# The S5 half of an output projection as seven block products instead of eight, its factors formed on the way

## The chip, the core and the metric

One Trainium2 chip, one core of it. The metric is the device time of one execution in microseconds (us), the median of several runs. The engines are PE (TensorE, matrix products), DVE (VectorE), ACT (ScalarE), POOL (GpSimd) and SP (SyncE, which here issues nearly all the DMAs). Each engine works through its own list of instructions in order, and semaphores make one wait for another.

## The reference, cut to what matters

One layer of a streaming encoder over 544 frames (512 of a new stream, 32 of a running one), width 2048, all in float32:

```python
h = rmsnorm(x, norm1_g)
q, f, i, g, u = split(h @ w_in)            # 4 x 1024 columns for HGRN2, 1024 for S5
o_h, S = hgrn_mixer(q, f, i, g, ...)       # 8 heads of 128, a gated linear recurrence
y = s5_ssm(u) ; hh = gelu(y)
o_s = hh * sigmoid(hh @ w_glu + b_glu)     # the GLU
mix = concatenate([o_h, o_s])              # 2048 channels
x = x + mix @ w_out                        # the output projection: (2048 x 2048)
x = x + square(relu(rmsnorm(x, norm2_g) @ w_ff1)) @ w_ff2
y = rmsnorm(x, final_norm_g)
```

The change is in `o_s @ w_out[1024:]`, the S5 half of the output projection: 1024 channels in, 2048 out.

## The kernel before

All products run transposed: channels lie on the 128 partitions and the frames along the free dimension, in two halves of 272 (`HALF`). A float32 product is made of three passes of the tensor engine: both factors are split into a rounded part and the rest (`hi` and `lo`), and `step` (L124 to L126) issues hi x hi, hi x lo and lo x hi, each 128 x 128 by 272 columns. A weight block is 128 x 1024 (eight K tiles for one block of 128 outputs): SP loads it (L88), ACT casts `hi` (L108) and DVE subtracts to `lo` (L109). Raw weights (`w`) and split ones (`hl`) have rings of two buffers each.

The stages, in order: input projection with the S5 and HGRN2 mixers woven into it; the GLU (eight blocks of 48 matmuls); the S5 half of the output projection (16 blocks of 48 matmuls, called here the S5 stage); the HGRN2 half (the HG stage, 16 blocks of 48); then the FFN, whose two products already use the seven-product scheme (`seven`, with eight PSUM banks).

In the GLU each block's result passes a sigmoid (ACT, L58) and a product with its input (DVE, L1001), and `split` (L184, L185) makes the pair of tiles that the S5 stage multiplies. In the S5 stage each block adds two PSUM banks to tiles `xr`, which hold the input x (L1019 loads, L1022 adds, L1023 stores to a buffer `x2` in HBM). The banks `g` are three.

Beside the S5 stage runs the last HGRN2 head (`hg_head`, head 7). Its matmuls are set between the products by `tick`, which counts pairs of K tiles, so that PE's order is fixed by the program; `manual_schedule` keeps PE to that order. The order on DVE, ACT and SP is made by a list scheduler when the program is built, by its own cost model, with priority for what stands in `with self.first()` (weights). Two steps of the head matter below: `kh` (L669 on DVE), which PE transposes (L679), and `ATs` (L792 on DVE), which PE multiplies (L802).

Before the HG stage the eight heads' outputs are loaded again (`mhl`, L1031, from buffers `mh` in HBM), cast (L1033) and subtracted (L1034) into the eight tiles `mix0` to `mix7`, the factors of that stage. `mhl` tiles come from a ring of four (`x_tile`). In the kernel before nothing else uses that ring in the S5 stage, and the tiles `xr` come from another one (`tt`). The last addition and the last stores of the S5 stage are put behind the first weights of the HG stage (`late_adds`, `stores`).

## Time and profile before

| | us |
|---|---|
| median of 3 runs | 2281.62 |
| the runs | 2277.82 to 2285.32 |
| span of the profiled execution (first to last instruction) | 2276.6 |
| PE busy in it | 2248.7 (99%) |
| DVE busy | 1799.9 (79%) |
| ACT busy | 1288.1 (57%) |
| the S5 stage, from the GLU's last matmul to the HG stage's first | 106.91 |
| of it, busy: PE, DVE, ACT | 106.91, 62.14, 43.51 |

The profiled execution's own time beyond its span is not listed; the median of the runs lies 5.0 us above that span. The profile is read by stages. A matmul's listed duration (about 290 ns) is longer than the distance to the next one (about 126 ns), since matmuls are pipelined, and the same holds in a smaller measure for DVE and ACT: what an instruction costs its engine in a dense stretch is the distance from its start to the next start.

### The profile page before, as it was taken

Reading aid. Unit: us, or ns where it says so; the run is one execution under the profiler, and the core shown is the slowest. Engines: PE = TensorE matmul, PEld = TensorE weight load, DVE = VectorE, ACT = ScalarE, POOL = GpSimd, SP = SyncE. Lnnn points to the kernel's source line nnn. Section 1 sums busy time; section 2 is a strip of 40 time slices with the busy share of each in tenths; the row PEclk is TensorE's granted clock in tenths of the full one; section 3 lists DMA queues with packets and bytes.
Section 4 is the critical chain, followed back from the end, with each engine's and each line's share of the span. In section 5 each row is a group of like instructions: output and inputs, shape, how many; then the busy total and the mean of one; then the engine's idle time right before and its main releaser. Section 6 shows DMA issues by size and latency. Waiting matters only on the chain.

```text
span 2276.6 us, 46775 instructions
## 1 busy us (share of the span) xinstructions
PE 2248.7 (99%) x19310; PEld 2225.2 (98%) x19310; DVE 1799.9 (79%) x2933; ACT 1288.1 (57%) x2259; POOL 39.1 (2%) x59
## 2 busy tenths in 40 slices
PE   8999999999999999999999999999999999999998
PEld 8999999999999999999999999999999999999997
DVE  7988889787657478777777777778888888888896
ACT  5655656564655256555555555556566565565574
POOL 0010001000000000000000000000000000000000
PEclk9999999999999999999999999999999999999999
DMA  5222232222345565445555544447554344344333
GB/s 195 88 83 92 88 91 87 81 84 86 119 146 177 161 201 173 146 157 166 179 169 171 177 147 154 145 143 257 169 173 162 109 164 163 111 162 168 107 103 107
DMA packets 139926, 322.12 MB, mean 141 GB/s; under 512 B 13344, under 2 KB 66336, under 8 KB 139712
## 3 DMA queue, kind: packets, MB, share of 16 engines
q1 hardware_dynamic: 139072, 316.90, 42.9%
q8 instruction: 151, 2.47, 0.5%
q10 hardware_dynamic: 640, 2.23, 0.3%
q14 instruction: 63, 0.52, 0.1%
HBM read 262.21 MB, written 56.87 MB: 140 GB/s over the span
## 4 chain that ended last, share of the span: by engine, by line
PE 90%; DVE 6%; ACT 3%; DMA 1%; issue 1%; SPq 0%; ACTq 0%; DVEq 0%
PE g L124 9%; PE g L126 9%; PE g L125 8%; PE bX L1134 8%; PE bX L1135 8%; PE bX L1136 8%; PE bE L1135 3%; PE bE L1134 3%; PE bC L1135 3%; PE bC L1134 3%; PE bD L1135 3%; PE bD L1134 3%; PE bF L1134 3%; PE bF L1135 3%; PE bD L1136 3%; PE bC L1136 3%
## 5 line engine op out<-in xcount | busy, mean ns | idle before, releaser
L124 PE MATMUL g<-a,hl 128*128 128x272 f32 x1648 | 491.0, 298 | 6.4 <-ACT hl L108 6.4
L126 PE MATMUL g<-a,hl 128*128 128x272 f32 x1648 | 476.0, 289 | 1.3 <-DVE hl L109 1.2
L125 PE MATMUL g<-a,hl 128*128 128x272 f32 x1648 | 475.0, 288 | 0.0
L109 DVE TENSOR_TENSOR hl<-w,hl 128x1024 fp32r<-128x1024 f32 (+3 forms) x348 | 383.5, 1111 | 112.7 <-ACT hl L108 112.2
L108 ACT CAST hl<-w 128x1024 fp32r<-128x1024 f32 (+3 forms) x348 | 334.5, 962 | 201.5 <-PE g L126 117.3
L109 DVE TENSOR_TENSOR hl<-s,hl 128x1024 fp32r<-128x1024 f32 x256 | 313.0, 1223 | 108.6 <-ACT hl L108 108.2
L108 ACT CAST hl<-s 128x1024 fp32r<-128x1024 f32 x256 | 268.7, 1050 | 179.1 <-PE bD L1136 97.9
L124 PEld LDWEIGHTS g<-a,hl 128*128 128x128 f32 x1648 | 311.6, 189 | 10.0 <-ACT hl L108 6.6
L126 PEld LDWEIGHTS g<-a,hl 128*128 128x128 f32 x1648 | 311.1, 189 | 2.3 <-DVE hl L109 2.3
L125 PEld LDWEIGHTS g<-a,hl 128*128 128x128 f32 x1648 | 311.0, 189 | 0.8 <-DVE a L188 0.5
L1135 PE MATMUL bX<-hf,hl 128*128 128x272 f32 x768 | 222.7, 290 | 0.0
L1134 PE MATMUL bX<-f,hl 128*128 128x272 f32 x768 | 222.3, 290 | 0.3 <-ACT hl L108 0.3
L1135 PE MATMUL bX<-f,hl 128*128 128x272 f32 x768 | 222.6, 290 | 0.0
L1134 PE MATMUL bX<-hf,hl 128*128 128x272 f32 x768 | 222.1, 289 | 0.5 <-ACT bD L1127 0.5
L1136 PE MATMUL bX<-f,hl 128*128 128x272 f32 x768 | 221.6, 289 | 0.7 <-DVE hl L109 0.7
L1136 PE MATMUL bX<-hf,hl 128*128 128x272 f32 x768 | 221.3, 288 | 0.0
L1136 PEld LDWEIGHTS bX<-f,hl 128*128 128x128 f32 x768 | 144.5, 188 | 1.0 <-DVE hl L109 1.0
L1134 PEld LDWEIGHTS bX<-hf,hl 128*128 128x128 f32 x768 | 144.7, 188 | 0.7 <-ACT bD L1127 0.7
L1134 PEld LDWEIGHTS bX<-f,hl 128*128 128x128 f32 x768 | 144.7, 188 | 0.6 <-ACT hl L108 0.5
L1136 PEld LDWEIGHTS bX<-hf,hl 128*128 128x128 f32 x768 | 144.5, 188 | 0.0
L1135 PEld LDWEIGHTS bX<-f,hl 128*128 128x128 f32 x768 | 144.4, 188 | 0.0
L1135 PEld LDWEIGHTS bX<-hf,hl 128*128 128x128 f32 x768 | 144.4, 188 | 0.0
(426 smaller groups left out, 5777.3 us busy)
## 6 DMA issues: line engine op xcount, KB each, us to landing
w<-w SPq DMA_DIRECT2D x256, 512.0 KB, 4.0
w<-wi SPq DMA_DIRECT2D x76, 512.0 KB, 3.4
hd<-ft SPq DMA_DIRECT2D x32, 952.0 KB, 4.7
hf<-hd SPq DMA_DIRECT2D x56, 544.0 KB, 6.6
w<-wo SPq DMA_DIRECT2D x32, 512.0 KB, 4.1
x<-x SPq DMA_DIRECT2D x32, 272.0 KB, 2.8
hhl<-hh SPq DMA_DIRECT2D x16, 274.0 KB, 3.5
x<-xT SPq DMA_DIRECT2D x16, 272.0 KB, 5.0
```

The lines of the kernel that those rows point to most:

```text
L108: self.nc.scalar.copy(hi[:, cols], w[:, cols])
L109: self.last_lo = self.nc.vector.tensor_sub(lo[:, cols], w[:, cols], hi[:, cols].bitcast(F32)).ins.name
L124: te.matmul(o, wh, xh, start=k == 0, stop=False)
L125: te.matmul(o, wh, xl, start=False, stop=False)
L126: te.matmul(o, wl, xh, start=False, stop=k == nk - 1)
L1134: nc.tensor.matmul(b[o], wh[:, s], xh, start=start and k == 0, stop=False, skip_group_check=True)
L1135: nc.tensor.matmul(b[o], wh[:, s], xl, start=False, stop=False, skip_group_check=True)
L1136: nc.tensor.matmul(b[o], wl[:, s], xh, start=False, stop=k == nk - 1, skip_group_check=True)
```

## The change

The 2048 outputs are taken in eight pairs of blocks and the 1024 channels in two halves of four K tiles. For each pair the two halves of the outputs, of the channels and of the frames make a 2 x 2 block product, which takes seven products of 4 K tiles (12 matmuls each) instead of eight:

- `right_forms` (in the GLU, for blocks 4 to 7) makes the seven right-hand factors from two GLU results: four subtractions (`forms`, L1123 to L1126 after) and seven splits (ACT L1010, DVE L1011), all of 272 columns. It replaces `split`, which made one pair of 544 columns for each of the eight blocks.
- `left_forms` makes four sums or differences of 512 columns of weights for each pair (L1143 to L1149) and splits three blocks of 1024 columns and one of 512.
- `seven_few` issues the products into three banks (X, F, C); ACT copies X into C or F three times per pair (L1168), and DVE adds to `xr` five times (L1162), one of these over both halves.
- `xr` now takes two tiles of the `x_tile` ring per pair, each for two blocks (loads L1051, stores L1057). The tiles `mix4` to `mix7` of the HG stage serve as raw weight and sum buffers meanwhile, and two tiles of ring `a` become a third split buffer `hl3`.
- The rest of head 7, its ticks and the loads of `mhl` (L1066), casts (L1068) and subtractions (L1069) stand as before in the source, behind the S5 stage.

```diff
+        def right_forms(k):
+            A, B = slice(0, HALF), slice(HALF, T)
+            x, y = mixs[k], mixs[k + 4]
...
+            fs = self.forms((x[:, A], x[:, B], y[:, A], y[:, B]),
+                            lambda: ms.tile([128, HALF], F32, tag="tt", name="tt", bufs=4))
+            for f, (z, pair, o) in enumerate(zip(fs, (ab, cd, cd, ef, gh, ef, gh), (o, A, B, A, A, B, B))):
+                hi, lo = pair[0][:, o], pair[1][:, o]
+                a.copy(hi, z)
+                v.tensor_sub(lo, z, hi.bitcast(F32))
+                mixf[f][k] = hi, lo
...
-            mixs.append(self.split(sg))
+            mixs.append(sg)
+            if m > 3:
+                right_forms(m - 4)
...
-        for m in range(NK):
-            x = [ms.tile([128, HALF], F32, tag="tt", name="xr", bufs=4) for _ in range(2)]
-            for h in range(2):
-                nc.sync.dma_start(x[h], d["xT"][:, m, HALF * h : HALF * h + HALF])
-            p = self.gemm([wo[m, 1]], mixs, (7,) if m == 0 else ())
...
+        self.rings["w"] = [0, [(lambda n: flat(mt(4 + n)), 2), (wpool, 2)]]
+        self.rings["s"] = [0, [(lambda n: flat(mt(6 + n)), 2)]]
+        self.rings["hl"] = [0, [(wpool, 2), (lambda n: hl3, 1)]]
+        for i in range(8):
+            m1 = 2 * i
+            xr = [x_tile("xr").rearrange("q (m t) -> q m t", m=2) for _ in range(2)]
             for h in range(2):
...
+                nc.sync.dma_start(xr[h], d["xT"][:, m1 : m1 + 2, HALF * h : HALF * h + HALF])
+            with self.first():
+                r1, r2 = self.load_raw(wo[m1, 1]), self.load_raw(wo[m1 + 1, 1])
+            self.seven_few(self.left_forms(r1, r2), mixf, 4, xr, adds if i == 7 else None)
+            for h in (1, 0):
+                for m in range(2):
+                    store = lambda m=m, h=h, xr=xr, m1=m1: nc.sync.dma_start(
+                        self.x2[m1 + m][:, HALF * h : HALF * h + HALF], xr[h][:, m])
+                    stores.append(store) if i == 7 else store()
+        self.rings = rings
...
+        def m12():
+            v.tensor_add(s12[:, L], r2[:, L], r2[:, H])
+            v.tensor_sub(s12[:, H], s12[:, L], r1[:, L])
+            return sp(s12)
+        def m34():
+            v.tensor_sub(s34[:, L], r1[:, L], r2[:, L])
+            v.tensor_sub(s34[:, H], r1[:, H], s12[:, H])
+            return sp(s34)
...
+        X, F, C = (self.gbank() for _ in range(3))
+        add = lambda o, p: v.tensor_add(o, o, p)
+        plan = ((X, True, None), (F, True, None), (X, False, C), (C, False, None), (X, False, F), (F, False, None),
+                (C, False, C))
+        for i, (o, start, copy) in enumerate(plan):
+            if copy is not None:
+                with self.first():
+                    a.copy(copy, X)
+            wh, wl = left[i]()
...
+            with self.first():
+                if i == 1:
+                    add(x[1], F.unsqueeze(1).broadcast_to([128, 2, HALF]))
+                if i == 3:
+                    add(x[0][:, 0], C)
+                if i == 5:
+                    add(x[1][:, 0], F)
```

PE's list has 96 matmuls of 272 columns fewer. First place, PE where it transposes `kh` of head 7 (`ps` are PSUM tiles), before; behind it goes on the second half of the stage's fourth block:

```order
L126 MATMUL g_9354<-a_9098,hl_9351 128x272
L679 MATMUL ps_9380<-cst1_193,kh_9149 128x128 [waits DVE_49]
L679 MATMUL ps_9380<-cst1_193,kh_9149 128x128 [waits Activation_49] x3
L689 MATMUL ps_9387<-cst1_193,kh_9149 32x128 [waits Activation_49]
L124 MATMUL g_9355<-a_8643,hl_9351 128x272
```

The same place on PE after; behind it starts the third pair (i = 2):

```order
L1175 MATMUL g_9372<-a_9156,hl_9463 128x272
L679 MATMUL ps_9478<-cst1_193,kh_9234 128x128 [waits DVE_49]
L679 MATMUL ps_9478<-cst1_193,kh_9234 128x128 [waits Activation_49] x3
L689 MATMUL ps_9485<-cst1_193,kh_9234 32x128 [waits Activation_49]
L1173 MATMUL g_9504<-a_8891,hl3_9179 128x272
```

Nothing moved here: 168 of the stage's matmuls stand ahead of this place in both lists, and 264 more between it and the product with `ATs` (L802).

Second place, DVE up to the subtraction for `kh` (L669), before:

```order
L109 TENSOR_TENSOR hl_9351<-w_9349,hl_9351 128x1024 [waits DMAHW4_49,Activation_49]
L659 TENSOR_TENSOR raw_8325<-raw_8325,e_9129 128x544 [waits DVE_49,Activation_49]
L1022 TENSOR_TENSOR xr_9282<-xr_9282,g_9291 128x272 [waits DMAHW5_49,DMAHW0_49,PE_49]
L663 SCALAR_TENSOR_TENSOR G_9142<-ones_108,raw_8325 128x128 [waits DVE_49]
L1034 TENSOR_TENSOR mix6_10439<-mhl_10437,mix6_10439 128x544 [waits DMAHW4_49,Activation_49]
L672 TENSOR_SCALAR nR_9157<-G_9142 128x4 [waits DVE_49]
L669 TENSOR_TENSOR kh_9149<-kh_9149,k_9130 128x544 [waits Activation_49]
```

Between the head's steps (L659, L663, L672, L669) stand here one weight block, one addition and one `mix` tile. The same place on DVE after (`mix6_9709` and `mix7_9710` are sums of weights for pair i = 3, `hl_9637` split weights of pair i = 2):

```order
L109 TENSOR_TENSOR hl_9637<-mix7_9503,hl_9637 128x1024 [waits Activation_49]
L1143 TENSOR_TENSOR mix6_9709<-w_9707 128x512 [waits DMAHW2_49,DVE_49]
L1148 TENSOR_TENSOR mix7_9710<-w_9705,w_9707 128x512 [waits DMAHW4_49,DVE_49]
L1144 TENSOR_TENSOR mix6_9709<-mix6_9709,w_9705 128x512 [waits DVE_49]
L653 TENSOR_TENSOR k_9215<-e_9214,raw_8325 128x544
L1149 TENSOR_TENSOR mix7_9710<-w_9705,mix6_9709 128x512 [waits DVE_49]
L658 TENSOR_SCALAR e_9214<-e_9214,hgp_527 128x544 [waits DVE_49,Activation_49]
L659 TENSOR_TENSOR raw_8325<-raw_8325,e_9214 128x544 [waits DVE_49,Activation_49]
L663 SCALAR_TENSOR_TENSOR G_9227<-ones_108,raw_8325 128x128 [waits DVE_49]
L672 TENSOR_SCALAR nR_9242<-G_9227 128x4 [waits DVE_49]
L669 TENSOR_TENSOR kh_9234<-kh_9234,k_9215 128x544 [waits Activation_49]
```

The head's steps moved behind the left factors of pairs 0 to 2 and the sums for pair 3: from the product with the last GLU result (L1021) to L669 DVE's list has 58 instructions, 7 of 1024 columns, 15 of 512, 12 of 544, 17 of 272, five scans and two small ones. From there to the step for `ATs` (L792) it has 73: 9 of 1024, 14 of 512, 5 of 544, 34 of 272 or 256, and 11 others.

Third place, SP at the end of the S5 stage, with the HG stage's first weights (`w_10480` and on), before:

```order
L1019 DMA xr_10338<-xT 128x272 [waits DMAHW6_49]
L88 DMA w_10480<-wo 128x1024 [waits DMAHW0_49,Activation_49]
L88 DMA w_10548<-wo 128x1024 [waits DMAHW1_49,DVE_49]
L88 DMA w_10635<-wo 128x1024 [waits PE_49]
L1023 DMA x214_98<-xr_10276 128x272 [waits DMAHW3_49,DVE_49]
```

Of the `mhl` loads six stand here some 75 rows earlier, in the GLU, and the last stands 17 rows ahead of `w_10480`. The same place on SP after, behind the stores of pair i = 6:

```order
L1066 DMA mhl_10469<-mh0_60 128x544 [waits DMAHW5_49,DMAHW4_49]
L1066 DMA mhl_10474<-mh1_61 128x544 [waits DMAHW6_49,DMAHW2_49,DMAHW0_49]
L1066 DMA mhl_10479<-mh2_62 128x544 [waits DMAHW7_49,DMAHW1_49,DVE_49]
L1066 DMA mhl_10484<-mh3_63 128x544 [waits DMAHW0_49,DVE_49]
L1066 DMA mhl_10489<-mh4_64 128x544 [waits DMAHW3_49,DMAHW1_49,DVE_49]
L88 DMA w_10542<-wo 128x1024
L88 DMA w_10610<-wo 128x1024
L88 DMA w_10697<-wo 128x1024 [waits PE_49]
L1066 DMA mhl_10494<-mh5_65 128x544 [waits DMAHW2_49,DVE_49]
L88 DMA w_10762<-wo 128x1024 [waits DMAHW4_49,DVE_49]
L88 DMA w_10849<-wo 128x1024 [waits DMAHW5_49,DVE_49]
L1066 DMA mhl_10499<-mh6_66 128x544 [waits DMAHW3_49]
```

All eight `mhl` loads moved to the end of the stage, and the first weights behind five of them. Of the ring's four tiles pair i = 7 holds two until its last stores, which stand behind all `mhl` loads, so that the eight loads pass through the other two: the first two wait for the stores of pair i = 6, each later one for the subtraction (L1069) of the load two before it.

## Rows read from the trace of the kernel before

**Rows 1.** The page: busy us (share of the span) and instructions of each engine.
```profile
PE 2248.7 (99%) x19310; PEld 2225.2 (98%) x19310; DVE 1799.9 (79%) x2933; ACT 1288.1 (57%) x2259; POOL 39.1 (2%) x59
```
**Rows 2.** Busy time by stretch (start:end and length, each engine, clock, DMA share, GB/s).
```profile
686.55:793.46 106.91, 106.91 (x1040) 104.92 (x1039) 62.14 (x113) 43.51 (x74) 0.00 (x0) 1.00 0.54 168
686.55:708.19 21.64, 21.64 (x176) 21.63 (x175) 18.90 (x33) 18.59 (x37) 0.00 (x0) 1.00 0.59 187
1640.00:1720.00 80.00, 80.00 (x636) 80.00 (x635) 70.00 (x97) 47.71 (x77) 0.00 (x0) 1.00 0.44 148
```
**Rows 3.** PE in order of time: start, length, engine, line, operation, out<-in.
```profile
689.94 0.60 PE L679 MATMUL ps<-cst,raw 128*128 128x128 f32 x4
...
708.19 0.60 PE L679 MATMUL ps<-cst,kh 128*128 128x128 f32 x4
...
749.86 0.40 PE L802 MATMUL ps<-ATs,vks 32*128 32x32 f32 x2
...
793.50 0.29 PE L124 MATMUL g<-mix,hl 128*128 128x272 f32 x1
```
**Rows 4.** ACT in order of time, end of the GLU.
```profile
686.75 1.05 ACT L108 CAST hl<-w 128x1024 fp32r<-128x1024 f32 x1 [1.41 <-PE g L126]
687.70 0.48 ACT L58 ACTIVATE sg<-g,cst 128x272 f32<-128x272 f32 x1
```
**Rows 5.** DVE in order of time: the last GLU result, then the head to `kh`.
```profile
687.83 1.23 DVE L109 TENSOR_TENSOR hl<-w,hl 128x1024 fp32r<-128x1024 f32 x1 [1.71 <-ACT hl L108]
688.97 1.26 DVE L1001 TENSOR_TENSOR sg<-sg,hhl 128x512 f32<-128x512 f32 x2
...
697.94 0.72 DVE L653 TENSOR_TENSOR k<-e,raw 128x544 f32<-128x544 f32 x1
698.58 1.35 DVE L1034 TENSOR_TENSOR mix<-mhl,mix 128x544 fp32r<-128x544 f32 x2
...
703.43 1.47 DVE L663 TENSOR_TENSOR_SCAN G<-ones,raw 128x128 f32<-128x128 f32 x5
...
705.51 0.71 DVE L669 TENSOR_TENSOR kh<-kh,k 128x544 f32<-128x544 f32 x1
```
**Rows 6.** DVE in order of time, second FFN product.
```profile
1999.62 0.43 DVE L1297 TENSOR_TENSOR acc<-acc,bX 128x272 f32<-128x272 f32 x1
1999.97 0.43 DVE L1297 TENSOR_TENSOR acc<-acc,bD 128x272 f32<-128x272 f32 x1
...
2006.04 0.68 DVE L1280 TENSOR_TENSOR s<-w 128x512 f32<-128x512 f32 x1
2006.64 0.69 DVE L1276 TENSOR_TENSOR s<-s,w 128x512 f32<-128x512 f32 x1
```
**Rows 7.** Instructions on `mhl` (count: duration ns min/median/max, first and last start); the load's landing.
```profile
L1033 ACT CAST mix<-mhl x8: 627/645/651, 676.1 to 769.1; 128x544 fp32r<-128x544 f32 x8
L1034 DVE TENSOR_TENSOR mix<-mhl,mix x8: 691/719/730, 678.1 to 769.8; 128x544 fp32r<-128x544 f32 x8
...
DMA to landing us min/median/max: 3.4/4.1/4.8
```
**Rows 8.** Loads of output projection weights, and their landing.
```profile
L88 SPq DMA_DIRECT2D w<-wo x32: 327/333/917, 671.0 to 862.0; - x32
...
DMA to landing us min/median/max: 3.4/4.1/5.9
```
**Rows 9.** Stores of `xr`, with the landing of all DMAs on `xr`.
```profile
L1023 SPq DMA_DIRECT2D x<-xr x32: 319/382/1915, 694.3 to 796.9; - x32
...
DMA to landing us min/median/max: 1.7/2.9/7.3
```
**Rows 10.** PE in order of time, at the first matmul and after waits at 25 us.
```profile
5.28 0.59 PE L124 MATMUL g<-a,hl 128*128 128x272 f32 x1 [5.28 <-ACT hl L108]
...
9.03 0.34 PE L126 MATMUL g<-a,hl 128*128 128x272 f32 x1
...
25.78 0.39 PE L126 MATMUL g<-a,hl 128*128 128x272 f32 x1 [0.68 <-DVE hl L109]
...
27.68 0.43 PE L124 MATMUL ps<-a,hl 128*128 128x272 f32 x1
...
29.26 0.43 PE L125 MATMUL g<-a,hl 128*128 128x272 f32 x1
```
**Rows 11.** Busy time by stretch, around the second of these places (0.66 is the granted clock).
```profile
25.00:30.00 5.00, 4.21 (x20) 3.79 (x20) 4.90 (x8) 2.85 (x6) 0.00 (x0) 0.66 0.55 157
```

More of the change, by code (lines that the diff above doesn't have):

```diff
@@ L97, in ring @@
             if turn < n:
-                return pool.tile(list(shape), dt, tag=tag, name=tag, bufs=n)
+                return pool(turn) if callable(pool) else pool.tile(list(shape), dt, tag=tag, name=tag, bufs=n)
             turn -= n
@@ L102, in pair @@
         t = self.ring("hl", (128, 2, 1024), F32R)
-        return t[:, 0], t[:, 1]
+        return t if isinstance(t, list) else (t[:, 0], t[:, 1])
     def split_w(self, w, t=None, cols=slice(0, 1024)):
@@ L1031, in mixers @@
             nc.sync.dma_start(t, self.mh[h])
-            z = ms.tile([128, 2, T], F32R, tag=f"mix{h}", name=f"mix{h}")
+            z = mt(h)
             a.copy(z[:, 0], t)
@@ L1092, in forms, with left_forms, part @@
         return b11, t1, t2, b21, t3, b22, t4
+    def left_forms(self, r1, r2):
+        v, sp = self.nc.vector, self.split_w
+        L, H = slice(0, 512), slice(512, 1024)
+        s12, s34 = self.ring("s"), self.ring("s")
+        memo = {}
+        def part(key, n, make):
+            if key not in memo:
+                with self.first():
+                    memo[key] = make()
+            return tuple(x[:, 512 * n : 512 * n + 512] for x in memo[key])
+        def m12():
[6 more added lines that the diff above has]
+            return sp(s34)
+        mr = lambda: sp(r1)
+        return (lambda: part("r", 0, mr), lambda: part("12", 0, m12), lambda: part("12", 1, m12),
+                lambda: part("r", 1, mr), lambda: part("34", 0, m34), lambda: part("34", 1, m34),
+                lambda: part("22", 1, lambda: sp(r2, None, H)))
@@ new lines, in seven_few, with end @@
+    def seven_few(self, left, right, nk, x, last):
+        a, v = self.nc.scalar, self.nc.vector
+        X, F, C = (self.gbank() for _ in range(3))
[7 more added lines that the diff above has]
+            wh, wl = left[i]()
+            for k in range(nk):
+                s = slice(128 * k, 128 * k + 128)
+                xh, xl = right[i][k]
+                self.nc.tensor.matmul(o, wh[:, s], xh, start=start and k == 0, stop=False, skip_group_check=True)
+                self.nc.tensor.matmul(o, wh[:, s], xl, start=False, stop=False, skip_group_check=True)
+                self.nc.tensor.matmul(o, wl[:, s], xh, start=False, stop=k == nk - 1, skip_group_check=True)
+                if k % 2:
+                    self.tick()
+            with self.first():
+                if i == 1:
[4 more added lines that the diff above has]
+                    add(x[1][:, 0], F)
+        def end():
+            return add(x[0][:, 1], C)
+        with self.first():
+            add(x[1][:, 1], X)
+            if last is None:
+                end()
+            else:
+                last.append(end)
```

16 lines of the change are left out of this document (12 added, 4 removed).

## The prediction

> **What bounds the kernel now.** I read the page first: PE is busy 99% of the span, DVE 79%, ACT 57% [rows 1], so a matmul that goes is worth its place on PE, as long as PE does not wait for something new. Then the S5 stage by itself: it lasts from 686.55 (27 matmuls of 0.126 us ahead of the head's first transposition at 689.94 [rows 3]) to 793.46, just ahead of the HG stage's first matmul at 793.50 [rows 3]. In these 106.91 us PE is busy throughout, DVE 62.14 and ACT 43.51 [rows 2]. PE is the bound and DVE has 45 us to spare, on average over the stage. But until the transposition of `kh` at 708.19 DVE is busy 18.90 of 21.64 us [rows 2, 3]: the dense part of head 7 lies there, and `kh` is done at 705.51 + 0.71 = 706.2 [rows 5], only 2.0 us ahead of PE's need for it. That place decides what the change is worth.
>
> **What it removes.** 768 - 672 = 96 matmuls of 272 columns. The nearest stretch with the same products (second FFN product, twelve matmuls each) has 636 in 80.00 us [rows 2], 0.1258 us each: **-12.1 us**. All 96 lie behind the product with `ATs`, since both places of the head keep their number of matmuls ahead of them (168, then 264 more). So PE needs `kh` 21.6 us after the stage's start and `ATs` 749.86 - 708.19 = 41.7 us later [rows 3], as before.
>
> **Prices on DVE.** Start to start, an operation of 272 columns takes 0.35 us, one of 512 columns 0.60 [rows 6], of 1024 1.14, of 544 between 0.63 and 0.70 (two `mix` tiles together 1.35), five scans 1.4 [rows 5]. I take 0.35, 0.60, 1.135 and 0.635.
>
> A rule of the Trainium skill can be held against these. The listed durations (0.43, 0.69, 1.23 us) are longer than the distances [rows 5, 6]. The Trainium skill ("VectorE: DVE Perf Modes", section on the TRN2 errata) prices a float32 tensor_tensor of N columns at (N + 151)/0.96 ns, that is 441, 691 and 1224 ns, which agrees with the durations. By it the 58 instructions of the next part would take an estimated 37 us instead of 32.1, and the time would be 5 us longer; the measured distance decides.
>
> **First stall, at `kh`.** In the GLU the forms keep DVE nearly full for the last three blocks (40 instructions: 3 x 1.135 + 3 x 0.60 + 31 x 0.35 + 3 x 0.2 = 16.7 us in three blocks of 48 x 0.126 = 6.03 us); PE does not wait for them there, cost 0, since the weights come first in the list. What comes after the last GLU result cannot start earlier than before: cast of the next split buffer (released by PE's last GLU matmul, 686.75 [rows 4]), the second sigmoid (687.70 [rows 4]), DVE's subtraction at 687.83 and its product at 688.97 [rows 5], 2.42 us into the stage. From that product to L669 DVE's new list has 58 instructions: 7 x 1.135 + 15 x 0.60 + 12 x 0.635 + 17 x 0.35 + 1.4 + 0.2 + 0.1 = 32.1 us. To these come waits inside the head's chain: from L653 to the end of L669 it lasted 697.94 to 706.22, 8.3 us [rows 5], while its own steps take 0.64 + 0.47 + 0.64 + 1.4 + 0.07 + 0.71 = 3.9 us on DVE; the rest was filled with other work, and now one addition of 0.6 us stands between them. That leaves 3.8 us at most idle, 0 if the chain's ACT steps come early; I take 3.0. So `kh` is ready at 2.42 + 32.1 + 3.0 = 37.5 us, and PE, which keeps its order, wants it at 21.6: **+15.9 us** (12.8 without the idle time; 18 with the upper idle time and an ACT list in which casts that wait for PE stand ahead of the head's steps). Part of it shows earlier, as short waits of the first pair for its last factors (K tile 3, made from the last GLU result). The head's DMAs and stores follow it and are not on the path.
>
> **Second stall, at `ATs`.** From L669 to L792 DVE's list has 73 instructions: 9 x 1.135 + 14 x 0.60 + 5 x 0.635 + 34 x 0.35 + 4 x 0.27 + 2 x 0.5 + 2 x 0.8 + some 1.0 = 38.4 us, against PE's 41.7 us. DVE is 92% full there and its additions wait for ends of products, copies X to C or F wait in ACT's list behind casts, and L792 stands behind three sums for the next pair (1.8 us). No row shows three banks with copies. With eight banks the same load per pair, 8.45 us of 10.56, cost no wait: PE is busy 80.00 of 80.00 us with DVE at 70.00 [rows 2]. That speaks for 0; five pairs with a wait of one 512-column sum and an addition each, 5 x 1.4, for 7. I take **+3**, nearer to the row of the second FFN product.
>
> **Third stall, at the HG stage.** The eight `mhl` tiles now pass through two buffers. Let 0 be the end of pair 6 on PE; pair 7 ends at 84 x 0.1258 = 10.6, and with the first half block of the HG stage, 24 matmuls, PE would be at 13.6. A store of `xr` lands 2.9 us after its issue [rows 9]; then the first `mhl` load (4.1), cast (0.65), subtraction (0.72) [rows 7]: done at 8.4. The third load waits for that and is done at 13.85. The fifth is issued then, and behind it in SP's list (an issue takes 0.33 [rows 8]) the first weights: landed at 14.2 + 4.1 [rows 8] = 18.3, cast behind `mix4`'s cast (18.6) in 1.05 [rows 4] to 19.65, subtraction to 20.8. The two next weight loads wait for the first two raw buffers (20.8 and 22.3, after the late addition), and the seventh and eighth `mhl` loads stand behind them: issued 22.7 and 23.0, landed 26.8 and 27.1, cast one after the other to 28.1, subtracted to 28.85. PE needs these for K tiles 6 and 7 of its first half block, done at 29.2 instead of 13.6: **+15.6 us**. With the shortest landings (1.7, 3.4 three times, 3.4) it is 11.6, with the longest of `mhl` and `w` (4.8, 5.9) 19.5 [rows 7 to 9].
>
> The Trainium skill has a lower price for a load ("DMA: Bandwidth & Descriptors", section on the anatomy of one DMA: a fixed 2.0 us plus bytes at 436 GB/s, there for another issuing engine). For 272 KB that is an estimated 2.6 us; three `mhl` loads and a weight load in the chain would then take about 5 us less, and the sum would be 5 us lower. The trace disagrees: its shortest `mhl` landing is 3.4 us [rows 7].
>
> **The clock.** After the wait at the start the first 14 distances take 9.03 - 5.28 = 3.75 us [rows 10] where 14 x 0.126 = 1.8: the lower of its two levels, 1.2 GHz. At 27.68 to 29.26, after waits of about 1 us, seven distances take 1.58 us [rows 10], and the granted clock of that stretch is 0.66 [rows 11]. A restart after a long wait so costs 1.4 to 2.0 us. Two restarts (at `kh` and at the HG stage): **+3.2** (0 if the clock holds, 5.6 with a third).
>
> **Edits with no price.** Left forms (4 x 0.60 per pair), a half more split, five additions: all in the DVE counts above. The copies on ACT (three per pair) are hidden by ACT's idle 63 us of the stage [rows 2]. The removed `split` of the GLU is on ACT and DVE beside PE. The FFN is untouched.
>
> **The sum.** -12.1 + 15.9 + 3 + 15.6 + 3.2 = +25.6 us. Against the profiled span of 2276.6 that is 2302.2, and with the 5.0 us by which the median lies above that span **2307 us**, 1.1% slower. The low ends give -12.1 + 12.8 + 0 + 11.6 + 0 = +12.3 (2294), the high ends -12.1 + 18 + 7 + 19.5 + 5.6 = +38 (2320).
>
> **Rivals.**
> - *The full saving:* the new work finds room and PE never waits: 2281.6 - 12.1 = 2269.5, faster. For it speaks that DVE has 45 us idle in the stage and gets some 37 us more; against it that 32.1 us of DVE work stand in a fixed list ahead of `kh` where PE has 21.6 us. It decides at 19.2 us for these 58 instructions, 0.33 us each, less than one of 272 columns takes. It would need the head's matmuls to come later or DVE to be much faster. Chance 0.04.
> - *Only the first stall:* the `mhl` chain is hidden, if loads land in about 1 us or PE is late enough: -12.1 + 15.9 + 3 + 1.7 = +8.5, 2290. Against it: each round is a load that has never landed in under 3.4 us [rows 7]. Chance 0.07.
> - *Only the HG stall:* the head is on time (DVE runs ahead in the GLU): -12.1 + 15.6 + 1.6 = +5.1, 2287, within 0.3%. Chance 0.06.
> - *Worse:* ACT's list, with casts that wait for PE ahead of copies that PE waits for, adds a wait to every pair, over 2320. Chance 0.03.
>
> **How the numbers follow.** The forecast (all three stalls) has 0.80. A measurement of this kernel tells about 0.3% (6.8 us) from no change. Slower by more: 0.80 + 0.07 + 0.03 = 0.90; within: 0.06; faster: 0.04. The range goes from 2290, which takes in the case of the first stall alone, to the high ends' 2320, and leaves out 0.13 and little more.
>
> **What would show it.** The S5 stage's PE list has 672 long matmuls. PE waits some 10 us or more in one piece on L679 for DVE's L669; DVE is busy nearly without a gap for the first 35 us of the stage; L802 waits a few us for L792. At the HG stage's start PE waits first for ACT's cast of the first weights, then for `mix6` and `mix7`, and these for `mhl` loads issued late; the granted clock drops after both. The prediction is wrong if PE reaches L679 with `kh` ready, if the `mhl` loads are issued before pair 6 ends, or if the stage up to the HG half's first half block lasts less than 110 us.

## The result, and the profile after

The changed kernel takes 2302.75 us (median of 4 runs, 2300.44 to 2308.14) beside 2279.85 for the kernel before (4 runs, 2277.82 to 2285.32; the first three of them have the median of 2281.62 from which the forecast starts): a ratio of 1.0097, 95% interval 1.0084 to 1.011, or 23 us more. The forecast was 2307, slower, with a range of 2290 to 2320.

First the page of the kernel after (engine, busy us, share of the span, instructions), which answers to [rows 1]:

```profile
span 2298.6 us, 46713 instructions
PE 2246.5 (98%) x19214; PEld 2219.8 (97%) x19214; DVE 1849.0 (80%) x3025; ACT 1313.3 (57%) x2319; POOL 39.0 (2%) x59
```

PE has 96 instructions fewer, as counted, DVE 92 more. The page says little else: a listed matmul is longer than its distance to the next, so that PE's busy time fell by 2.2 us only. The places say more. Here are the busy times of the kernel after by stretch (columns as in [rows 2]): from the S5 stage's first matmul to the transposition of `kh`, from there to the product with `ATs`, to the last pair's end, and to the end of the HG stage's first half block.

```profile
685.15:724.18 39.03, 24.50 (x175) 23.30 (x174) 36.42 (x65) 24.52 (x48) 0.00 (x0) 0.87 0.41 132
724.18:769.66 45.48, 43.77 (x521) 41.65 (x521) 38.92 (x74) 23.38 (x46) 0.00 (x0) 0.96 0.45 139
769.66:801.52 31.86, 31.84 (x248) 31.37 (x248) 24.22 (x38) 15.96 (x25) 0.00 (x0) 1.00 0.39 126
801.52:818.07 16.55, 7.74 (x27) 5.96 (x26) 6.55 (x9) 5.32 (x7) 0.00 (x0) 0.65 0.81 273
```

The same four stretches of the kernel before, from [rows 3] and the end of its first half block at 796.50, last 21.64, 41.67, 43.60 and 3.04 us.

| place | before | after | difference | forecast |
|---|---|---|---|---|
| to `kh` | 21.64 | 39.03 | +17.4 | +15.9 |
| `kh` to `ATs` | 41.67 | 45.48 | +3.8 | +3, and half of the clock's 3.2 |
| `ATs` to the stage's end | 43.60 | 31.86 | -11.7 | -12.1 |
| first half block of the HG stage | 3.04 | 16.55 | +13.5 | +15.6, and the other half |
| the next 167 matmuls | 20.87 | 21.76 | +0.9 | (in that half) |
| together | 130.82 | 154.68 | +23.9 | +25.6 |

So the gain came nearly whole (11.7 of 12.1 us), and the two waits at `kh` and at the HG stage cost 2.6 times as much (17.4 + 13.5). The profiled spans of different kernels can't be compared to the microsecond, since what lies ahead of the S5 stage differs from run to run (its first matmul starts between 685.15 and 691.29 us in the traces here, at 686.55 before). All comparisons below therefore use the stretch of the last line, from the S5 stage's first matmul to the HG stage's 192nd: 130.82 us before, 154.68 after. In all fourteen kernels the median of the runs is 2148 to 2152 us more than this stretch.

PE's waits in the S5 stage after (waiting tile and line, who released it, us in total, times, longest):

```profile
PE ps L679 <- DVE kh L669: 11.3, 1, 11.3
PE g L1174 <- DVE a L1011: 2.2, 2, 1.4
PE ps L802 <- DVE ATs L792: 1.3, 1, 1.3
PE g L1175 <- DVE hl L109: 1.1, 1, 1.1
PE ps L799 <- ACT hgAT L787: 0.4, 1, 0.4
```

And DVE in order of time between the last GLU result and `kh` (start, length, engine, line; in brackets idle time and who ended it):

```profile
688.00 1.09 DVE L1021 TENSOR_TENSOR sg<-sg,hhl 128x512 f32<-128x512 f32 x1
...
717.04 0.72 DVE L653 TENSOR_TENSOR k<-e,raw 128x544 f32<-128x544 f32 x1
...
719.22 0.56 DVE L658 TENSOR_SCALAR e<-e,hgp 128x544 f32<-128x544 f32 x1 [0.86 <-ACT raw L655]
720.59 0.73 DVE L659 TENSOR_TENSOR raw<-raw,e 128x544 f32<-128x544 f32 x1 [0.81 <-ACT raw L58]
721.35 1.49 DVE L663 TENSOR_TENSOR_SCAN G<-ones,raw 128x128 f32<-128x128 f32 x5
...
723.40 0.73 DVE L669 TENSOR_TENSOR kh<-kh,k 128x544 f32<-128x544 f32 x1 [0.48 <-ACT kh L58]
```

The 58 instructions take 688.00 to 724.13, 36.1 us, some 2.4 of them idle in the head's own chain. PE had been waiting since 712.9. Against [rows 5] the head's own steps did not get slower: from L653 to the end of L669 they last 7.1 us, 8.3 before. They begin later.

The start of the HG stage after, PE and ACT in order of time:

```profile
806.60 0.59 PE L124 MATMUL g<-mix,hl 128*128 128x272 f32 x1 [4.93 <-ACT hl L108]
...
814.67 0.64 ACT L1068 CAST mix<-mhl 128x544 fp32r<-128x544 f32 x1 [3.88 <-DMA mhl<-mh]
...
815.36 0.60 PE L124 MATMUL g<-mix,hl 128*128 128x272 f32 x1 [2.95 <-ACT mix L1068]
```

The DMA issues on SP, which say why (start, time until the last of the group is issued, line):

```profile
792.74 8.90 SPq L1066 DMA_DIRECT2D mhl<-mh  x5
801.69 1.37 SPq L88 DMA_DIRECT2D w<-wo  x3
803.45 0.33 SPq L1066 DMA_DIRECT2D mhl<-mh  x1
807.83 3.01 SPq L88 DMA_DIRECT2D w<-wo  x2
810.90 1.00 SPq L1066 DMA_DIRECT2D mhl<-mh  x2
```

Five `mhl` loads trickle through two buffers for 8.9 us, the HG stage's first weights stand behind them until 801.69, when PE has just ended the last pair, and the last two `mhl` loads stand behind weights that wait for their own buffers until 810.90.

The clock: PE's granted clock is 0.50, the lower of its two levels (1.2 GHz), in this stretch after the two waits:

```profile
810.00:820.00 10.00, 6.56 (x24) 5.25 (x23) 3.10 (x5) 1.94 (x3) 0.00 (x0) 0.50 0.65 213
```

Matmuls lie 0.23 us apart there, where 0.126 is usual. Such slow stretches of 10 to 12 matmuls stand at 692, 726, 808 and 818 us, each behind a wait or a group of short ones; 1.0 to 1.2 us each.

### The profile page after: what moved, and what is told of

Its sections match the earlier page's. It is cut to its first block, busy times and chain, and to the rows that moved or that the text cites. A ratio compares the mean times of both kernels' runs of the same rounds, so it can differ in the third digit from the quotient of the medians.

```text
span 2298.6 us, 46713 instructions
## 1 busy us (share of the span) xinstructions
PE 2246.5 (98%) x19214; PEld 2219.8 (97%) x19214; DVE 1849.0 (80%) x3025; ACT 1313.3 (57%) x2319; POOL 39.0 (2%) x59
## 3 DMA queue, kind: packets, MB, share of 16 engines
q1 hardware_dynamic: 138816, 316.90, 41.8%
## 4 chain that ended last, share of the span: by engine, by line
PE 86%; DVE 7%; ACT 3%; DMA 2%; issue 1%; SPq 0%; ACTq 0%; DVEq 0%
PE bX L1235 8%; PE bX L1236 8%; PE bX L1237 8%; PE g L124 7%; PE g L126 7%; PE g L125 7%; PE bE L1236 3%; PE bC L1236 3%; PE bE L1235 3%; PE bC L1235 3%; PE bD L1236 3%; PE bD L1235 3%; PE bF L1235 3%; PE bF L1236 3%; PE bD L1237 3%; PE bE L1237 3%
## 5 line engine op out<-in xcount | busy, mean ns | idle before, releaser
L109 DVE TENSOR_TENSOR hl<-w,hl 128x1024 fp32r<-128x1024 f32 (+2 forms) x340 | 371.7, 1103 | 109.7 <-ACT hl L108 108.5
L124 PE MATMUL g<-a,hl 128*128 128x272 f32 x1392 | 415.9, 299 | 6.4 <-ACT hl L108 6.4
L108 ACT CAST hl<-w 128x1024 fp32r<-128x1024 f32 (+2 forms) x340 | 324.4, 955 | 163.9 <-PE g L126 83.0
L126 PE MATMUL g<-a,hl 128*128 128x272 f32 x1392 | 402.0, 289 | 1.3 <-DVE hl L109 1.2
L125 PE MATMUL g<-a,hl 128*128 128x272 f32 x1392 | 401.1, 288 | 0.0
L124 PEld LDWEIGHTS g<-a,hl 128*128 128x128 f32 x1392 | 263.1, 189 | 9.5 <-ACT hl L108 6.6
L126 PEld LDWEIGHTS g<-a,hl 128*128 128x128 f32 x1392 | 262.8, 189 | 2.2 <-DVE hl L109 2.0
L125 PEld LDWEIGHTS g<-a,hl 128*128 128x128 f32 x1392 | 262.7, 189 | 0.6 <-DVE a L188 0.2
```

Of the source, the lines that this page charges most:

```text
L108: self.nc.scalar.copy(hi[:, cols], w[:, cols])
L109: self.last_lo = self.nc.vector.tensor_sub(lo[:, cols], w[:, cols], hi[:, cols].bitcast(F32)).ins.name
L124: te.matmul(o, wh, xh, start=k == 0, stop=False)
L125: te.matmul(o, wh, xl, start=False, stop=False)
L126: te.matmul(o, wl, xh, start=False, stop=k == nk - 1)
```

## The experiments

Each kernel is the changed one with the edit shown. The table puts them together; the ratio is to runs of the kernel before on the same chip.

| kernel | median | ratio (95%) | stretch |
|---|---|---|---|
| before | 2279.85 to 2282.94 | 1 | 130.82 |
| after | 2302.75 | 1.0097 (1.0084 to 1.011) | 154.68 |
| e1_hand_over | 2291.26 | 1.004 (1.0024 to 1.0055) | 142.87 |
| e2_head_first | 2299.78 | 1.0078 (1.0063 to 1.0093) | 150.75 |
| e3_both | 2288.95 | 1.0032 (1.002 to 1.0044) | 138.66 |
| e4_no_head | 2282.05 | 0.9999 (0.9989 to 1.0008) | 133.05 |
| e5_forms_first | 2288.80 | 1.003 (1.0018 to 1.0042) | 139.08 |
| e6_sums_on_pool | 2293.78 | 1.0048 (1.0033 to 1.0063) | 141.88 |
| e7_sums_on_pool_only | 2301.24 | 1.0081 (1.0064 to 1.0097) | 151.35 |
| e8_head_later | 2290.26 | 1.0034 (1.0022 to 1.0046) | 139.04 |
| e9_head_later_only | 2292.06 | 1.005 (1.0032 to 1.0069) | 142.30 |
| e10_head_all_first | 2284.88 | 1.0019 (1.001 to 1.0028) | 135.02 |
| e11_no_sums | 2274.11 | 0.9967 (0.9954 to 0.998) | 125.77 |
| e12_no_sums_change | 2284.36 | 1.0018 (1.0009 to 1.0028) | 134.46 |

### The hand-over to the HG stage

The heads' outputs are loaded into the tile that later holds `lo`, and no longer through the ring `x_tile`:

```diff
-            t = x_tile("mhl")
-            nc.sync.dma_start(t, self.mh[h])
             z = mt(h)
+            t = z[:, 1].bitcast(F32)
+            nc.sync.dma_start(t, self.mh[h])
             a.copy(z[:, 0], t)
             v.tensor_sub(z[:, 1], t, z[:, 0].bitcast(F32))
```

> The change with one edit: the eight heads' outputs are loaded straight into the second half of their own tiles mix0 to mix7, not through the ring that the tiles xr also use. The S5 stage itself is untouched. Theory (the ring and SP's list behind it make the wait at the HG stage): PE starts the HG stage within 3 us of the end of the last pair and does its first half block without waits; of the 14.4 us that this place costs after the change (from 801.52 to the first second-half matmul at 818.07, 3.0 us of it being the half block itself, and 0.9 us of slow clock behind), 11 to 14 go: 2289 to 2292 us. Rival (the loads' own landing or the last head's late store make the wait, not the ring): PE still waits 6 us or more for mix6, mix7 or the first weights, at most 6 us go: 2297 to 2303 us.

The theory's time came: 11.5 us went (the stretch: 11.8). Of PE's waits at the HG stage these are left:

```profile
PE g L124 <- ACT hl L108: 1.1, 1, 1.1
PE g L126 <- DVE hl L109: 0.7, 1, 0.7
```

The wait at `kh` is 11.3 us as before the edit, so the two places do not depend on each other. The ring and SP's list behind it made the wait; neither the landing of a load nor the late head did.

### The order on DVE

The dense part of head 7 gets the weights' priority (e2; e3 has e1's edit besides), and then the last right factors too (e5, with e1's edit):

```diff
+        up = ExitStack()
+        if h == 7:
+            up.enter_context(self.first())
         e, k = tmp("e"), self.hone("k")
...
         v.tensor_mul(kh, kh, k)
         tact(EG, G, AF.Exp)
+        up.close()
...
-            if m > 3:
+            if m == 7:
+                with self.first():
+                    right_forms(3)
+            elif m > 3:
                 right_forms(m - 4)
```

> The change with one edit: the dense part of head 7 (up to the product kh) has the weights' priority in the list scheduler, so that DVE has 33 instructions instead of 52 from the product with the last GLU result's end to kh, and the left factors of pairs 2 and 3 stand behind it. No instruction is added or removed. Theory A (only the order on DVE is at fault at kh): PE waits under 4 us for kh where it waited 11.3, and nothing else becomes late: 2289 to 2293 us. Theory B (DVE's amount up to ATs is too large in any order: 32 + 38 us of work behind the first 2.4 us against 63.3 us on PE): the wait at kh goes but 6 to 10 us of waiting come back at the factors of pairs 2 to 5 or at ATs: 2295 to 2301 us.

> Both edits together. If the two places are independent, the gains add: with theory A of the head 2275 to 2280 us, faster than or equal to the kernel before; with theory B 2283 to 2289 us. If a wait of the S5 stage only moves to the HG stage, no better than 2290 us.

> The two edits of before (loads of the heads' outputs into their own tiles, dense part of head 7 first) and one more: the factors made from the last GLU result (K tile 3) have the weights' priority too. With the two edits PE waits 3.57 us at 706.8 for the last of these factors, whose subtraction stood behind the head's steps and the left factors, and then runs 13 matmuls at the lower clock. Theory A (order alone): this wait and its slow stretch go and nothing takes their place: 2283 to 2286 us against 2289. Theory B (DVE has too much to do up to ATs in any order): the waits at KQ (3.9 us) or ATs (1.3 us) grow by as much: 2287 to 2291 us.

Counted as instructions DVE has 37 instead of 58 ahead of `kh` (the expectation counted rows, where equal neighbours are one). The wait at `kh` is gone in all three kernels, and theory A was wrong. The longest of PE's waits in the S5 stage with both edits (e3):

```profile
PE g L1178 <- DVE a L1015: 4.4, 2, 3.6
PE b L727 <- DVE KQ L749: 3.9, 1, 3.9
```

and with the last right factors first as well (e5):

```profile
PE b L765 <- DVE KQ L749: 4.3, 1, 4.3
PE g L1180 <- ACT g L1175: 1.7, 1, 1.7
PE b L727 <- DVE KQ L749: 1.7, 1, 1.7
PE g L1182 <- DVE hl L109: 1.4, 2, 0.9
...
PE g L1180 <- ACT a L1014: 1.2, 1, 1.2
```

Each time the longest wait is removed, most of its microseconds come back as several shorter ones, mostly at whatever DVE now does last; in e5 2.9 us of them are put down to ACT, at a copy of a bank (L1175) and a cast of right factors (L1014). In all PE waits 16.2 us in the S5 stage after the change, 11.5 in e2, 11.1 in e3 and 12.7 in e5. Of 11.3 us at `kh` some 3 to 4 were won (e2 3.0 us by the medians, 3.9 by the stretch), and e5 won nothing over e3. The times of e2, e3 and e5 are those of theory B.

### Without head 7

```diff
-        self.spawn(0, self.hg_head(7, q, f, vv, g))
+        self.hg_out()
+        S0 = self.small.tile([128, 128], F32, tag="S0", name="S0", bufs=2)
+        nc.sync.dma_start(S0, d["st_h"][7])
+        nc.sync.dma_start(d["o_hs"][7], S0)
+        nc.sync.dma_start(self.mh[7], vv)
```

> The change without the rest of head 7: its output and its states are not computed (raw tiles are stored in their place), everything else stands as after the change, with the late loads of mhl too. The head's matmuls take 10.3 us of PE in the stage before (106.91 us less 768 x 0.1258), so these go as well. Theory (kh and ATs are the only places where PE waits in the S5 stage; pairs of products by themselves are fed in time): 2302.7 - 17.4 - 3.9 - 10.3 = 2271 us, PE waits in all under 3 us from pair 1 to pair 7. Rival (three banks with copies and sums make PE wait in every pair): PE waits 5 us or more at the pairs' products, 2276 us or more.

The theory's 2271 did not come: 2282 is a time of the rival, but not for the rival's reason. From the second pair (i = 1) on PE waits for nothing, as the theory had it:

```profile
712.00:784.40 72.40, 72.40 (x580) 72.29 (x578) 60.17 (x90) 32.53 (x51) 0.00 (x0) 1.00 0.57 179
```

The pairs by themselves are fed, with three banks and three copies each, and DVE is 83% busy (60.17 of 72.40) without any head. What the expectation missed is the first pair: before 712 us PE waits 4.3 us for the factors that are made from the last GLU result and for the first left factors, and 33 matmuls follow these waits at the lower clock, some 3.3 us. It had put these into the head's 17.4 us. They belong to the products, whose factors come straight out of the GLU's last block; after the change they stand ahead of the wait at `kh`, and without them PE would have come there earlier and waited longer. From the last pair to the end of the stretch e4 takes 1.0 us more than the kernel after (39.45 against 38.44).

### The sums of weights on POOL

`m12` and `m34` issue their four operations on POOL (`nc.gpsimd`), with e5's edits (e6) or with e1's alone (e7):

```diff
-            v.tensor_add(s12[:, L], r2[:, L], r2[:, H])
-            v.tensor_sub(s12[:, H], s12[:, L], r1[:, L])
+            g = self.nc.gpsimd
+            g.tensor_add(s12[:, L], r2[:, L], r2[:, H])
+            g.tensor_sub(s12[:, H], s12[:, L], r1[:, L])
```

> As before, and the four sums or differences of weights of each pair on POOL, which is idle in this stage (2% busy over the span): 32 instructions of 512 columns, 19.2 us at 0.60 us each, leave DVE's list. Theory B (DVE's amount is what delays head 7): the waits at KQ and ATs shrink to under 2 us together, 2278 to 2283 us. Rival (these operations take so long on POOL, in a chain of two per factor, or slow DVE beside them, that the left factors come late): PE waits at the pairs' products, 2286 us or more; POOL's durations in this trace show which.

> The change with the loads of the heads' outputs into their own tiles (2291 us), and the sums of weights on POOL, with the head's priority as the change has it. Of the 52 to 58 DVE instructions ahead of kh some 10 are such sums, 6 us at 0.60. Theory B (the wait at kh is DVE's amount ahead of it): the wait there falls from 11.3 to 5 to 6 us, 2284 to 2287 us. Rival (POOL is slow or slows DVE): the wait at kh stays within 2 us of 11.3, 2289 us or more.

The rival held: 5 us slower than e5, 10 slower than e1. In e7 DVE has 46 instructions ahead of `kh` instead of 58, with 2.1 us idle among them, and still ends `kh` 41.8 us into the stage, where e1 ends it at 39.0. POOL in e6, one group of four sums:

```profile
722.27 1.30 POOL L1151 TENSOR_TENSOR mix<-w 128x512 f32<-128x512 f32 x1 [7.28 <-DVE hl L109]
723.65 2.15 POOL L1152 TENSOR_TENSOR mix<-mix,w 128x512 f32<-128x512 f32 x1
725.76 1.77 POOL L1157 TENSOR_TENSOR mix<-w 128x512 f32<-128x512 f32 x1
727.50 1.85 POOL L1158 TENSOR_TENSOR mix<-w,mix 128x512 f32<-128x512 f32 x1
```

and DVE in the same microseconds:

```profile
720.92 1.22 DVE L109 TENSOR_TENSOR hl<-mix,hl 128x1024 fp32r<-128x1024 f32 x1
722.06 0.43 DVE L1171 TENSOR_TENSOR xr<-xr,g 128x272 f32<-128x272 f32 x1
722.55 2.11 DVE L109 TENSOR_TENSOR hl<-mix,hl 128x1024 fp32r<-128x1024 f32 x1
724.59 1.80 DVE L823 SCALAR_TENSOR_TENSOR rawg<-rawg,cst,r 128x544 f32<-128x544 f32 x1
726.31 1.25 DVE L676 TENSOR_SCALAR nR<-G 128x4 f32<-128x4 f32 x1
727.48 0.71 DVE L824 TENSOR_TENSOR o<-o,rawg 128x544 f32<-128x544 f32 x1
```

The subtraction of 1024 columns takes 2.11 us beside POOL and 1.22 just ahead; `nR`, four columns, 1.25 where it takes 0.17 in the kernel after. The Trainium skill ("SBUF — State Buffer", section "SBUF: two separate sides") has a rule for this: a DVE instruction with two operands in SBUF, or in a mode that uses two ports, and a POOL instruction that reads SBUF take a shared pair of ports in turn, each for its whole length. The stretched rows with two operands in SBUF agree with it: the subtraction of 2.11 us ends 1.09 us after POOL's first sum (723.57 to 724.66), and POOL's three later sums end 1.14, 1.14 and 1.16 us after the DVE instruction beside them (724.66, 726.39, 728.19). So do the additions to `xr`, whose second operand lies in PSUM: 23 of them in e6 have a mean of 0.43 us, as without POOL. `nR`, which has one operand, ends 0.03 us after POOL's third sum; whether it is of the rule's second kind no run shows.

### Head 7 at a later place on PE

e8 puts `kh` 36 and `ATs` 78 matmuls later, with e5's edits; e9 puts the whole head 144 matmuls later, with e1's alone; in both K tile 7 comes last in the HG stage's first block. e10 adds to e8 priority for the products KQ and for `nR`, and puts the load of `mix7` behind the first weights.

```diff
-        for n, (nm, src, wait) in enumerate((("vT", vv, 3), ("kT", kh, 16 if h < 7 else 24))):
+        for n, (nm, src, wait) in enumerate((("vT", vv, 3), ("kT", kh, 16 if h < 7 else 30))):
...
-            yield 5
+            yield 5 if h < 7 else 6
...
-        yield 8
+        yield 8 if h < 7 else 9
...
+            if h == 7:
+                up.enter_context(self.first())
             r0 = self.htmp("r0")
...
-                p = self.gemm([wo[m, 0]], mixh, (), late_adds)
+                p = self.gemm([wo[m, 0]], mixh, (7,) if m == 0 else (), late_adds)
```

In e9 the first of these has 48, and of the others only the last is there. What e10 adds:

```diff
         def level(hs):
+            with self.first() if h == 7 else ExitStack():
+                return level_(hs)
+
+        def level_(hs):
...
         def late_adds():
+            while mix7:
+                self.after(mix7.pop(0)(), self.last_load, "weights first")
             while adds:
...
+            if h < 7:
+                load()
+            else:
+                mix7.append(load)
```

> The three edits (loads into their own tiles, head 7's dense part first, last right factors first), and the places of head 7 in PE's list later: kh 36 matmuls later, ATs 78 (9.8 us); its last steps get priority on DVE, and K tile 7 comes last in the first block of the HG stage. Nothing is added or removed on DVE. Theory B (DVE's amount ahead of each place of the head is what PE waits for, so that the same amount against a later place costs nothing): the waits at KQ (4.3 and 1.7 us), ATs (1.3) and the stretch at the lower clock (1.4) go, 2280 to 2284 us, and 2 to 5 us of waits of the first pair stay. Rival (the head's end is then late: its output's store, its load and mix7 stand at the HG stage's start): PE waits 5 us or more there, 2286 to 2290 us.

> The change with the loads into their own tiles (2291 us), and only kh and all that follows of head 7 later in PE's list, by 144 matmuls (18.1 us); K tile 7 last in the first block of the HG stage; DVE's priorities as the change has them. Theory B: the wait at kh (11.3 us) and its slow stretch (1.4 us) go; at the HG stage up to 5 us come back, since only 12 us of products are left behind ATs where the head's last steps, its store and its load took some 20: 2278 to 2285 us. Rival (the wait at kh belongs to the order, not to the place): PE waits for kh or for KQ again, 2287 us or more.

> The kernel with the head later (2290 us), and two more edits: all of head 7's products with decays (KQ) and its step nR have the weights' priority on DVE and ACT, and the load of mix7 and what follows it stand behind the first weights of the HG stage. There PE waited 4.3 us for KQ, whose second half stood 5.4 us behind the first on DVE with left factors between, then ran 21 matmuls at the lower clock (2.1 us), and 3.0 us at the HG stage, whose first weights were issued at 796.4 behind the load of mix7, with 17 slow matmuls (1.7 us). Theory (order and places can be set so that DVE's amount costs PE nothing but the first pair's waits): both waits and their slow stretches go, 2279 to 2283 us, level with the kernel before. Rival (DVE's amount: what the head gains the left factors lose): PE waits at the pairs' products or at the HG stage again, 2286 us or more.

e9 is a miss for theory B (2292.06 us, where it had 2278 to 2285), and tells the most. PE wants `kh` 18.1 us later, but DVE delivers it 10 us later too: L669 starts at 739.40, 48.2 us after the stage's first matmul, where it was 38.2 after the change. The list scheduler used the room: 76 instructions instead of 58 stand ahead of `kh`, since the left factors go first wherever they can.

```profile
739.40 0.73 DVE L669 TENSOR_TENSOR kh<-kh,k 128x544 f32<-128x544 f32 x1 [0.33 <-ACT kh L58]
```

PE still waits 3.1 us for `kh`, 3.4 for KQ in two pieces and 3.6 at the HG stage, with 13, 16 (behind the second piece) and 19 slow matmuls behind these waits, and the stretch is that of e1.

```profile
PE ps L679 <- DVE kh L669: 3.1, 1, 3.1
```

e8 came at the rival's time as well: the longer wait at KQ, which was to go by theory B, stays at 4.3 us. It won 3.5 us in the S5 stage (109.2 us from its first to its last matmul, 112.7 in e5) and gave it back at the HG stage, where the head's last steps now end:

```profile
PE b L765 <- DVE KQ L749: 4.3, 1, 4.3
PE g L124 <- ACT hl L108: 3.0, 1, 3.0
```

e10 removes both, and is the fastest kernel that computes all: 2284.88 us, still 0.19% slower than before. It lies between the two theories. What it wins over e8 is at the HG stage: its S5 stage takes 108.6 us, 0.6 less than that of e8, since three waits stand where the one at KQ was:

```profile
PE b L727 <- DVE qf L764: 1.7, 1, 1.7
PE ps L807 <- ACT hgAT L795: 1.6, 1, 1.6
PE ps L810 <- DVE ATs L800: 1.3, 1, 1.3
```

In all PE waits 9.5 us in nine pieces in the S5 stage (the longest 1.7, for a copy of a bank on ACT), and in the stretch with the head DVE is busy 57.03 of 58 us. Here it is (columns as in [rows 2]: PE, weight loads, DVE, ACT):

```profile
712.00:770.00 58.00, 53.70 (x614) 51.36 (x612) 57.03 (x102) 28.99 (x48) 0.00 (x0) 1.00 0.60 184
```

### DVE's amount alone

The last two leave out the sums, with nothing in their place, on e10 (e11) and on e1 (e12), so that they do not compute the layer:

```diff
-            v.tensor_add(s12[:, L], r2[:, L], r2[:, H])
-            v.tensor_sub(s12[:, H], s12[:, L], r1[:, L])
-            return sp(s12)
+            return sp(r2)
...
-            v.tensor_sub(s34[:, L], r1[:, L], r2[:, L])
-            v.tensor_sub(s34[:, H], r1[:, H], s12[:, H])
-            return sp(s34)
+            return sp(r1)
```

> The kernel with head 7 first and later (2284.9 us) without the four sums or differences of weights of each pair: the raw blocks are split in their place, so the output projection's S5 half is not what the reference asks for. PE's list, the splits, the loads and the additions are the same; only 32 instructions of 512 columns, 19.2 us, leave DVE. Theory B (DVE's amount is the bound of the stretch with the head, 57.0 of 58 us busy there): PE's waits inside that stretch (qf 1.7, hgAT 1.6, ATs 1.3) shrink and about 5 us go, 2278 to 2281 us, under the kernel before. Rival (PE waits for chains of steps between DVE and ACT, not for DVE's amount): no more than 2 us go, 2283 us or more.

> The change with the loads into their own tiles (2291.3 us) without the same sums (the S5 half of the output projection is wrong in the same way). Ahead of kh DVE's list has 11 instructions of 512 columns fewer (6.6 us) and one of 544 more (0.6). Theory B: the wait at kh falls from 11.3 to 5 to 6 us, and ATs follows, 2283 to 2286 us. Rival (the head's own chain of steps sets kh, and the rest only fills its gaps): the wait at kh stays over 9 us, 2288 us or more.

e11 takes 2274.11 us, 10.8 less than e10 and 0.33% less than before (interval 0.2 to 0.46%). That is twice the 5 us of the expectation: PE's waits in the whole S5 stage fell from 9.5 to 2.8 us, not only those beside the head. With PE's list unchanged DVE is at 47.61 us between 712 and 770 us, and PE at 57.61:

```profile
712.00:770.00 58.00, 57.61 (x647) 55.51 (x646) 47.61 (x88) 34.20 (x67) 0.00 (x0) 1.00 0.59 189
```

Its S5 stage starts 5.8 us later in the trace than that of e10 (691.08 and 685.31 us); in the same part of the stage, 717.77 to 775.77, DVE is busy 44.93 us and PE all 58.00. The waits at `qf`, `hgAT` and `ATs` are gone; the longest that are left in the S5 stage are

```profile
PE g L1195 <- DVE hl L109: 1.4, 2, 0.9
PE g L1193 <- ACT g L1188: 1.2, 2, 0.8
```

e12 came at its forecast time, though its wait at `kh` fell less than theory B had it:

```profile
PE ps L679 <- DVE kh L669: 7.4, 1, 7.4
```

The waits for right factors ahead of it fell too (from 2.2 us to 0.2), so that PE came to `kh` 3.2 us earlier and waited longer there; `kh` itself ends 32.0 us into the stage instead of 39.0 (e1), some 7 us earlier for 6 us or a little more of work that left the list ahead of it (47 instructions instead of 58). So it is DVE's amount of work ahead of the head's places that PE waits for. Without the sums the left factors are also split straight from the loaded weights, two steps sooner; other DVE work of the same length was not taken out to tell this apart.

## Why the prediction was right

**The bound.** It said that PE bounds the stage on average, that DVE is nearly full until `kh`, and that this place decides. It did: PE waits 11.3 us there in one piece.

**The saving** of 12.1 us is 11.7 where it falls, behind `ATs`.

**The first stall** was sized at 15.9 us from 58 instructions at 32.1 us, 3.0 us idle, and a start 2.42 us into the stage. Measured: a start at 2.85, 36.1 us with some 2.4 idle, so that the instructions took 33.7, 5% more than priced. The prices by distance were the better ones: the Trainium skill's formula ("VectorE: DVE Perf Modes", section on the TRN2 errata) gave an estimated 37. So the place cost 17.4 us, 1.5 more than the forecast: the instructions took 1.6 more and the start came 0.4 later, with 0.6 less idle. It was also said that a part would show earlier, as waits of the first pair: 1.07, 0.83 and 1.38 us. That these waits are not the head's, and stay when the head is gone (e4), was not said.

**The second stall** was taken as 3 between 0 and 7, nearer to the second FFN product's row. The restart of the clock behind `kh` falls here too, so that 4.6 us stood against this place, and it costs 3.8: 1.7 us of waits (`ATs` 1.3, `hgAT` 0.4) and some 1.7 of slow clock behind `kh`, 1.1 in the products and the rest in the transpositions. The reason given, additions and copies in the pairs, is not what was seen: the pairs behind the first wait for nothing (e4), and the waits lie in the head's own chain. That the size is near is luck. In other kernels PE does wait for a copy of a bank, 1.7 us in e5, e8 and e10 and 5.2 in e7.

**The third stall** was the right mechanism, 2.8 us too large with its clock share (14.4 against 17.2). The mis-sized term is the load: `mhl` was taken to land in 4.1 us [rows 7], and after the change the landings are

```profile
DMA to landing us min/median/max: 2.7/2.9/6.7
```

The first five, issued one by one, landed in 2.7 to 3.0 us, and the last three, issued among weight loads, in 3.8 to 6.7. So the first weights were issued 10.7 us after the end of pair 6, where 14.2 was worked out, and part of this was lost behind them. The reason for the shorter landings was not tested. The Trainium skill's price ("DMA: Bandwidth & Descriptors", section on the anatomy of one DMA, there for another issuing engine), which gave an estimated 2.6 us and against which the shortest landing before spoke, is near those of the first five; a duration from the trace of another stretch was not the better price for them. The chain from load to load was as told: five loads, weights, two more.

**The clock** was 3.2 us for two restarts. There were four slow stretches of matmuls, 4.3 us in all, the additional ones behind the first pair's waits, where it cost nothing since PE had to wait for `kh` anyway, and between the HG stage's two waits.

The sum erred by 1.7 us over the stretch (25.6 against 23.9). The places erred by up to 2.8 us and in both directions, so that so close a sum is in part luck. The forecast of 2307 us lies 4 us above the median: besides the sum, the rest of the profiled execution was 1.9 us shorter after the change (2298.6 - 154.68 against 2276.6 - 130.82), and the median lies 4.15 us above the span, not 5.0.

**The rivals.** The full saving was put at 0.04, since 58 instructions at the prices seen do not fit into 19.2 us. The runs sharpen this: another order has only 37 of them ahead of `kh` (e2), and order and places can win much back, but e10, with the head's steps first and their places later, is still 4.2 us behind in the stretch. "Only the first stall" describes a kernel that can be made: e1, 2291.3 us where 2290 was worked out. e2 was the try at "only the HG stall": the head is on time, but 2299.8 us came where 2287 was worked out, since other waits took the place of that at `kh`.

## What to carry to other kernels

A scheme that takes products from PE and adds sums elsewhere is to be weighed on the engine that makes the factors, in the fullest part of the stage and not over its mean: here DVE had 45 us idle in the stage before and, in the best order that was found (e10), 1 of 58 us where the last head runs beside it, and only with 19 us of sums taken away (e11, no longer the same result) did the saved products show as time. When a wait is removed by order and most of its microseconds come back in smaller waits elsewhere, look at the amount of work of the engine behind it; a later place for the waiting instruction, by itself, let the scheduler put more ahead of it (e9). When tiles that are held long move into a ring that another stage uses for its first loads, look at who stands behind those loads in the issuing queue: this hand-over alone cost 11.5 us, and loading straight into the tile of destination gave it back.

## What the runs showed of the hardware

POOL at 2% busy is not a free engine beside DVE: a sum of 512 columns takes 1.26 to 1.29 us there with none of DVE's two-operand work in SBUF beside it (e6, 769 to 774 us) and up to 2.3 otherwise (3.2 for the first in e7), against 0.68 on DVE, or 0.60 from start to start; and beside it DVE's instructions on SBUF operands take up to twice their time and more (2.11 for 1.22 us, 1.25 for 0.17), while those with an operand in PSUM do not (0.43). The rows of e6 show the two engines taking turns. So 19.2 us taken from DVE's list made the kernel 5 to 10 us slower.

A wait on PE can cost 0.4 to 0.9 of its length again through the clock: in e9 waits of 3.1, 1.8 and 3.6 us are followed by 13, 16 and 19 matmuls at the lower clock, 1.3 to 1.9 us each time at 0.1 us per matmul. Not every wait is: behind one of 1.7 us in e10, at 709 us, one matmul is late and the next ones lie 0.126 us apart.
